# The convolution of a two-layer trunk: the four-token products moved behind the first rows' gates, gates fixed among the taps, six diagonal taps, and empty products in the norm's wait

## The chip, the core and the metric

The kernel runs on one core of a Trainium2 chip. Five engines work beside each other, each through its own queue and in that queue's order: PE (matrix products; its weight loads are shown as PEld), DVE (vector), ACT (scalar), POOL (GpSimd) and SP, which issues most of the transfers. They wait for each other through semaphores only. The time is that of the whole program on the device, in microseconds (us). Three runs of the kernel before took 942.58, 945.01 and 945.92 us; the median, 945.01 us, is the time before.

## The reference, cut to what matters

The program is a two-layer encoder trunk on 256 tokens of 1024 channels in float32. Each layer is a half-weighted gated feed-forward part, a token mixer, and a second such part. The mixer of layer 0 is a convolution module, the only part that the change touches:

```python
def conv_module(h, w_pw1, w_dw, g_norm, w_pw2):
    u = h @ w_pw1
    a, b = jnp.split(u, 2, axis=-1)
    u = a * jax.nn.sigmoid(b)
    u = lax.conv_general_dilated(          # causal, depthwise, 31 taps
        u, w_dw[:, None, :].astype(u.dtype), window_strides=(1,),
        padding=[(CONV_WIDTH - 1, 0)], ...
        feature_group_count=D_MODEL)
    u = jax.nn.silu(rmsnorm(u, g_norm))    # the norm runs over the 1024 channels
    return u @ w_pw2
```

The norm of a token needs all 1024 channels of that token, so nothing behind the norm can start before the slowest channel is convolved.

## The kernel before

**Tiles.** Channels lie on the 128 partitions: eight channel tiles, numbered 0 to 7, each 128 channels by 256 tokens. The tokens are two "rows blocks" of 128, called first rows (tb = 0) and second rows (tb = 1). `V` holds the gated input of the taps, `Y` their sum, `Z` the normed and activated result, and `o` the last product.

**The stage, in order.** `conv_in` goes through a list `steps` of (tile, tokens): tiles 0 and 1 first rows, 0 and 1 second rows, tiles 2 to 5 all tokens, then tiles 6 and 7 first rows, 6 and 7 second rows. A step is two groups of eight matmuls (`gate`, then `u`, line 730), a sigmoid of `gate` on ACT (`sg`, line 739) and a multiplication on DVE (line 750) that writes `V`. I call that multiplication the tile's gate. The four PSUM banks of the tag "A" hold `gate` and `u` in turn, so a step's products also wait until older banks are read.

**The 31 taps** are shared out by the tables `CONV_DVE`, `CONV_POOL` and `CONV_PE` at the head of the file; an entry is (tile, first tap, end, which rows). On DVE a tap is one multiply-add into one of two PSUM accumulators (`acc`, lines 818 and 820), on POOL it is a product on ACT (`prod`, line 845) and an addition on POOL (line 846), with six `prod` buffers between the two engines. On PE a tap is a product with a diagonal matrix of the tap's weights (`taps_pe`, line 856, out `y`); those matrices are made by ACT during the first feed-forward part. Tile 4 takes another way, here called the four-token products: DVE writes its gated input `vq` in four phases (line 743), a transfer stores it to DRAM, four more fetch it back as `VQ` in another layout, and PE does 36 matmuls of 64 columns (`quad`, line 757). Their result goes back through DRAM in the same manner (`yq`, then `YQ`).

**The norm.** For each tile ACT squares `Y` (`square`, `sq`), and PE sums over channels with one-column products (`total`, `ms`). `normed` then runs a chain over four engines: DVE scales the mean (`msc`, line 891), POOL takes the power (`rc`, line 893), ACT makes a diagonal matrix (`dg`, line 895), PE spreads it (`rb`, line 897), DVE multiplies (`z`, line 903), ACT activates (`Z`, line 905), and the last products `o` follow (line 981, and lines 277, 280, 281 for the tiles whose weights are split in two parts). This is done for the first rows, and for the second rows in the middle of the first rows' last products.

**What sets the order.** The program is written with a scheduling layer that places each engine's instructions by its own estimate of time. `order(a, b)` forces b ahead of a on one engine, and functions marked `urgent` are placed ahead of others. The order on each engine is fixed when the program is built.

Of the kernel before, what the change touches and what calls it, by code (L numbers as in the profile page):

```python
# [11 lines left out]
F32 = mybir.dt.float32  # L12
# [7 lines left out]
P = 128  # L20
# [66 lines left out]
def trunk(ctx: ExitStack, tc: tile.TileContext, x, xt, pos, invf, gains, gfin, wdw, wq,  # L87
# [619 lines left out]
    def conv_in(act, X, make_next):  # L707
# [26 lines left out]

        @urgent
        def glu(i, t, gate, u):
# [3 lines left out]
            if i == CONV_QUAD:  # L740
                v = act.tile([P, PH, QT], F32, tag="vq", name="vq")
                by_phase = lambda a: a.rearrange("p (t f) -> p f t", f=PH)
                nc.vector.tensor_mul(v, by_phase(u[:, t]), by_phase(sg[:, :n]))
# [6 lines left out]
            nc.vector.tensor_mul(V[:, i, PAD + t.start:PAD + t.stop], u[:, t], sg[:, :n])  # L750
# [13 lines left out]
        def back(b):  # L764
# [5 lines left out]
            for g in range(4):  # L770
                nc.sync.dma_start(YQ[32 * g:32 * g + 32], dv[g])

# [13 lines left out]
        for n, (i, t) in enumerate(steps):  # L786
# [8 lines left out]
            if i == CONV_LAST[0] - 1:  # L795
                before = quad(mm)
        last_product = before
# [9 lines left out]
        slot = [0]  # L807

        def taps_dve(k, j0, j1, t, after={}):

            slot[0] ^= 1
            c = slice(slot[0] * S, slot[0] * S + t.stop - t.start)
            out = Y[:, k, t]
            for j in range(j0, j1):
# [6 lines left out]
                if j in after:  # L821
                    order(ins, after[j].ins)
# [7 lines left out]
        def taps_pool(k, j0, j1, t):  # L830
# [3 lines left out]
            if k not in odd:  # L834
                odd[k] = act.tile([P, S], F32, tag="odd", name=uid("odd"))
            y = [(part[k] if k in part else Y[:, k, :])[:, t], odd[k][:, t]]
            for j in range(j0, j1):
# [4 lines left out]
                else:  # L842
# [3 lines left out]
                    nc.gpsimd.tensor_tensor(o, o, p, op=ALU.add)  # L846
            nc.gpsimd.tensor_tensor(y[0], y[0], y[1], op=ALU.add)

        def taps_pe(t, done):

            b = bank("A", "y")
            y = {}
            for i, (k, j0, j1) in enumerate(CONV_PE):
                y[k] = b[:, i * P:(i + 1) * P]
                for j in range(j0, j1):
                    mm = nc.tensor.matmul(y[k], diag[k][:, j - j0, :], V[:, k, j + t.start:j + t.stop],
                                          start=(j == j0), stop=(j == j1 - 1))
                    done.append(mm)
            return y

# [27 lines left out]
        def normed(tb, after=()):  # L888
# [4 lines left out]
            nc.gpsimd.tensor_tensor(rc, ms, neghalf, op=ALU.pow)  # L893
            dg = act.tile([P, P], F32, tag="dg", name=uid("dg"), bufs=2)
            nc.scalar.activation(dg, ident, AF.Copy, scale=rc)
# [13 lines left out]
            return on_dve[0], zi  # L909

        halves = (tbs(0), tbs(1), every)
        for items, taps in ((CONV_DVE, taps_dve), (CONV_POOL, taps_pool)):
            for k, j0, j1, half in items:
                if half is not None:
                    taps(k, j0, j1, halves[half])
# [470 lines left out]
```

## Time and profile before

| | |
|---|---|
| median of three runs | 945.01 us |
| the profiled execution's own time | 945.98 us |
| its span (first to last instruction) | 944.2 us |
| mean granted clock of PE | 0.987 |
| PE busy | 924.9 us, 98% |
| DVE, ACT, POOL busy | 679.8, 533.1, 220.4 us |
| convolution stage, from its first product to the first product of the next part | 187.3 to 305.0 us |

Times in rows of the profile are microseconds from the span's start. A row of the timeline gives the start, the time until its last instruction ends, the engine, the line, the operation, what it writes and reads, the shape, and how many records were merged; in brackets stands how long the engine had been idle just before and what ended that wait. A float32 matmul of lines 730, 757, 856, 875 and 981 leaves two records. A row of the stage table gives a stretch, its length, then for each of PE, PEld, DVE, ACT and POOL the busy time with the number of records, then the clock granted to PE (1.00 is full speed, 0.50 half), the share of the transfer engines that was busy, and GB/s.

### The profile page before, as it was taken

How to read it: one execution, taken by the hardware profiler on the slowest of the kernel's cores; microseconds unless marked ns; L12 is line 12 of the kernel's file. 1: busy time of each engine (PE TensorE's matmuls, PEld its weight loads, DVE VectorE, ACT ScalarE, POOL GpSimd, SP SyncE). 2: the span in 40 equal slices, each digit the busy share in tenths (PEclk: the TensorE clock that was granted, in tenths of full speed). 3: DMA queues.
4: the chain of work that ended last, by engine and by line, in shares of the span. 5: the costliest groups of instructions: out<-in, count | busy, mean ns of one | idle time of the engine just before them, and what ended most of it. 6: DMA issues, size and time to landing. Idle time of an engine off the chain costs nothing.

```text
span 944.2 us, 12585 instructions
## 1 busy us (share of the span) xinstructions
PE 924.9 (98%) x4401; PEld 769.6 (82%) x4401; DVE 679.8 (72%) x1042; ACT 533.1 (56%) x927; POOL 220.4 (23%) x337
## 2 busy tenths in 40 slices
PE   8999999998989999999999999999999999999997
PEld 6888887897966888888778888888888778888886
DVE  5866877689665766777786767779675566666875
ACT  6754546478375645546564554554765575454652
POOL 1102232379560000123130102222300001003223
PEclk9999999999789999999999999999999999999999
DMA  9985656666024677655658765667451547675651
GB/s 342 358 288 179 223 158 222 230 218 234 22 90 177 228 242 240 226 164 201 227 205 311 251 226 183 191 211 257 158 222 62 179 166 258 224 249 164 203 209 45
DMA packets 61983, 194.46 MB, mean 206 GB/s; under 512 B 12384, under 2 KB 34784, under 8 KB 42208
## 3 DMA queue, kind: packets, MB, share of 16 engines
q1 hardware_dynamic: 61344, 192.98, 59.2%
q8 instruction: 34, 0.56, 0.2%
q10 hardware_dynamic: 576, 0.69, 0.2%
q14 instruction: 29, 0.24, 0.1%
HBM read 180.79 MB, written 12.85 MB: 205 GB/s over the span
## 4 chain that ended last, share of the span: by engine, by line
PE 69%; DMA 10%; DVE 9%; ACT 4%; issue 4%; POOL 3%; SPq 1%; POOLq 0%; ACTq 0%; DVEq 0%
PE u L277 15%; PE u L281 15%; PE u L280 15%; DVE lo L168 4%; PE o L277 4%; PE o L280 4%; PE o L281 4%; DMA raw<-in_f1w 3%; POOL sums L178 3%; DMA gb<-gd 2%; PE o L981 2%; DMA raw<-in_f2w 2%; PE quad L757 1%; ACT hi L167 1%; DVE lo L187 1%
## 5 line engine op out<-in xcount | busy, mean ns | idle before, releaser
L168 DVE TENSOR_TENSOR lo<-raw,hi 128x1024 fp32r<-128x1024 f32 (+1 forms) x250 | 302.4, 1244 | 81.7 <-ACT hi L167 81.2
L167 ACT CAST hi<-raw 128x1024 fp32r<-128x1024 f32 (+1 forms) x250 | 247.7, 1046 | 152.2 <-PE u L281 107.0
L277 PE MATMUL u<-lo,Xh 128*128 128x512 f32 x688 | 268.1, 390 | 0.7 <-DVE lo L168 0.7
L281 PE MATMUL u<-hi,Xl 128*128 128x512 f32 x688 | 267.8, 390 | 0.9 <-DVE Xl L336 0.9
L280 PE MATMUL u<-hi,Xh 128*128 128x512 f32 x688 | 267.7, 389 | 0.0
L281 PEld LDWEIGHTS u<-hi,Xl 128*128 128x128 f32 x688 | 129.1, 188 | 28.7 <-DVE Xl L336 1.7
L277 PEld LDWEIGHTS u<-lo,Xh 128*128 128x128 f32 x688 | 129.1, 188 | 28.1 <-DVE lo L168 1.1
L280 PEld LDWEIGHTS u<-hi,Xh 128*128 128x128 f32 x688 | 129.1, 188 | 26.4
L277 PE MATMUL o<-lo,Gh 128*128 128x512 f32 (+1 forms) x236 | 91.6, 388 | 1.6 <-DVE lo L168 1.5
L178 POOL TENSOR_TENSOR sums<-raw 128x1024 f32<-128x1024 f32 x20 | 53.3, 2665 | 162.4 <-DMA raw<-in_f2w 43.6
L280 PE MATMUL o<-hi,Gh 128*128 128x512 f32 (+1 forms) x236 | 91.0, 386 | 0.0
L281 PE MATMUL o<-hi,Gl 128*128 128x512 f32 (+1 forms) x236 | 91.0, 386 | 0.0
L617 POOL TENSOR_TENSOR sx<-gb 128x128 f32<-128x128 f32 x20 | 12.1, 603 | 316.7 <-DMA gb<-gd 316.7
L609 ACT CAST Gh<-gb 128x512 fp32r<-128x512 f32 (+2 forms) x48 | 25.7, 538 | 63.7 <-DMA gb<-gd 63.7
L186 ACT CAST hi<-sums 128x1024 fp32r<-128x1024 f32 x40 | 41.2, 1052 | 32.5 <-PE u L281 13.6
L187 DVE TENSOR_TENSOR lo<-sums,hi 128x1024 fp32r<-128x1024 f32 x40 | 56.1, 1434 | 0.0
L610 DVE TENSOR_TENSOR Gl<-gb,Gh 128x512 fp32r<-128x512 f32 (+2 forms) x48 | 33.2, 704 | 31.6 <-ACT Gh L609 31.6
L277 PEld LDWEIGHTS o<-lo,Gh 128*128 128x128 f32 x236 | 44.3, 188 | 12.4 <-DVE lo L168 3.7
L281 PEld LDWEIGHTS o<-hi,Gl 128*128 128x128 f32 x236 | 44.3, 188 | 9.0
L280 PEld LDWEIGHTS o<-hi,Gh 128*128 128x128 f32 x236 | 44.3, 188 | 8.6
L820 DVE SCALAR_TENSOR_TENSOR acc<-V,dw,acc 128x128 f32<-128x128 f32 (+1 forms) x153 | 50.2, 401 | 0.0
L845 ACT ACTIVATE prod<-V,dw 128x128 f32<-128x128 f32 (+1 forms) x131 | 47.0, 410 | 3.0 <-POOL odd L846 1.5
(254 smaller groups left out, 1345.2 us busy)
## 6 DMA issues: line engine op xcount, KB each, us to landing
raw<-in_f2w SPq DMA_DIRECT2D x66, 1024.0 KB, 5.0
raw<-in_f1w SPq DMA_DIRECT2D x64, 1024.0 KB, 5.3
raw<-in_cw SPq DMA_DIRECT2D x12, 1024.0 KB, 6.3
gd<-gt SPq DMA_DIRECT2D x160, 64.0 KB, 2.8
gb<-gd SPq DMA_DIRECT2D x40, 256.0 KB, 2.9
raw<-in_wo SPq DMA_DIRECT2D x4, 1024.0 KB, 5.4
raw<-in_wuq SPq DMA_DIRECT2D x3, 1024.0 KB, 4.8
WQ<-in_wq SPq DMA_DIRECT2D x1, 2304.0 KB, 9.2
```

The costliest lines, as they stand in the source:

```text
L167: behind(nc.scalar.copy(hi[:, c], raw[:, c]))
L168: behind(nc.vector.tensor_sub(lo[:, c], raw[:, c], hi[:, c].bitcast(F32)))
L178: behind(nc.gpsimd.tensor_tensor(t[:, 0:2, :], v[:, 0:4:3, :], v[:, 1:2, :].to_broadcast([P, 2, 512]), op=ALU.add))
L186: behind(nc.scalar.copy(hi[:, c0:c1], x[:, c0:c1]))
L187: behind(nc.vector.tensor_sub(lo[:, c0:c1], x[:, c0:c1], hi[:, c0:c1].bitcast(F32)))
L277: mm = nc.tensor.matmul(o, ah, bl, start=start, stop=False)
L280: nc.tensor.matmul(o, ah, bh, start=False, stop=False)
L281: return nc.tensor.matmul(o, al, bh, start=False, stop=stop)
L609: nc.scalar.copy(dh, x)
L610: nc.vector.tensor_sub(dl, x, dh.bitcast(F32))
L820: ins = nc.vector.scalar_tensor_tensor(out if j == j1 - 1 else y, v, w, y, op0=ALU.mult, op1=ALU.add)
L845: last_prod[0] = nc.scalar.activation(p, v, AF.Copy, scale=w)
```

## The change

Five things are changed, all within the convolution stage:

1. The 36 four-token products stand behind the products of tiles 6 and 7 for the first rows, where they stood ahead of them. The six diagonal taps of tile 6 for the first rows follow them at once.
2. The tables are new. Tile 0's first rows go to DVE whole (31 taps, 22 before), and POOL's nine taps of it with the addition that joined them are gone. Tile 7 has no diagonal taps any more: DVE takes 23 taps and POOL 8 in the first rows, DVE all 31 in the second. PE keeps the six diagonal taps of tile 6. ACT makes six diagonal matrices instead of twelve.
3. `CONV_GATES` ties three gates to places among DVE's taps: the gate of tile 4 ahead of tap 22 of tile 2, those of tiles 6 and 7 (first rows) ahead of taps 10 and 18 of tile 5.
4. `filled` issues 12 empty products (zeros, bfloat16, 256 columns) between the first rows' sums and `rb`, and 6 between `rb` and the last products.
5. In the second rows, ACT's products from the seventh tap on stand behind `dg`, and their additions on POOL behind `rc`. The two accumulators are no longer used in alternating halves, and tiles 6 and 7 have a second buffer for POOL's odd taps.

On PE, from the last products of tile 5 on (`gate_1837`, `u_1838`), before:

```order
L730 MATMUL u_1838<-Xp_1535,raw_1782 128x256 x8
L757 MATMUL quad_1858<-VQ,WQ 128x64 x36
L730 MATMUL gate_1903<-Xp_1535,raw_1805 128x128 x8
L730 MATMUL u_1904<-Xp_1535,raw_1805 128x128 x8
L730 MATMUL gate_1924<-Xp_1535,raw_1835 128x128 x8
L730 MATMUL u_1925<-Xp_1535,raw_1835 128x128 x8
```

and now (`u_1831` is tile 5's):

```order
L732 MATMUL u_1831<-Xp_1528,raw_1775 128x256 x8
L732 MATMUL gate_1851<-Xp_1528,raw_1798 128x128 x8
L732 MATMUL u_1852<-Xp_1528,raw_1798 128x128 x8
L732 MATMUL gate_1872<-Xp_1528,raw_1828 128x128 x8
L732 MATMUL u_1873<-Xp_1528,raw_1828 128x128 x8
L761 MATMUL quad_1893<-VQ,WQ 128x64 x36
L793 MATMUL y_1938<-V,diag_445 128x128 x6
L732 MATMUL gate_1945<-Xp_1528,raw_1798 128x128 x8
```

Four groups of products now stand between tile 5 and the four-token products, and the first rows' diagonal taps have moved up from the end of the stage.

On PE at the norm of the first rows (`ms_2511` and `ms_2514` are the first rows' sums), before:

```order
L856 MATMUL y_2538<-V,diag_445 128x128 x6
L856 MATMUL y_2538<-V,diag_518 128x128 x6
L875 MATMUL ms_2511<-ones,sq_2552 128x1
L875 MATMUL ms_2511<-ones,sq_2555 128x1
L897 MATMUL rb_2565<-dg_2563,ones 128x128
L981 MATMUL o_2697<-raw_1989,Z 128x512
```

and now, up to the first of the empty products:

```order
L793 MATMUL y_2528<-V,diag_445 128x128 x6
L896 MATMUL ms_2514<-ones,sq_2510 128x1
L896 MATMUL ms_2516<-ones,sq_2510 128x1
L896 MATMUL ms_2514<-ones,sq_2512 128x1
L896 MATMUL ms_2514<-ones,sq_2536 128x1
L896 MATMUL ms_2516<-ones,sq_2512 128x1
L896 MATMUL ms_2514<-ones,sq_2539 128x1
L782 LDWEIGHTS still
L782 MATMUL y_2528<-still 128x256
```

The squares of the four-token tile (`sq_2510`) and of tiles 5, 6 and 7 are now summed right behind the second rows' diagonal taps; eleven more empty products, `rb` and six more follow ahead of `o`.

On ACT around the first rows' diagonal matrix, before:

```order
L845 ACTIVATE prod_2690<-V,dw 128x128
L845 ACTIVATE prod_2693<-V,dw 128x128
L895 ACTIVATE dg_2563<-ident,rc_2561 128x128
L905 ACTIVATE Z<-z_2567,G 128x128
L905 ACTIVATE Z<-z_2570,G 128x128
```

and now:

```order
L743 ACTIVATE sg_1984<-gate_1966 128x128
L830 ACT_TABLE_LOAD
L830 ACTIVATE silu_1987<-neghalf 128x1
L890 ACTIVATE sq_2510<-YQ 128x256
L890 ACTIVATE sq_2512<-Y 128x256
L890 ACTIVATE sq_2536<-Y 128x128
L890 ACTIVATE sq_2539<-Y 128x128
L916 ACTIVATE dg_2559<-ident,rc_2557 128x128
L876 ACTIVATE prod_2647<-V,dw 128x128
L876 ACTIVATE prod_2650<-V,dw 128x128
L876 ACTIVATE prod_2653<-V,dw 128x128
L876 ACTIVATE prod_2656<-V,dw 128x128
```

Three more such products follow, and only then the first `Z`: seven products of the second rows have moved from ahead of `dg` to a place between it and `Z`, and the last gate's sigmoid and the table load now stand directly ahead of the four squares.

The diff, cut to its core:

```diff
-CONV_DVE = ((0, 0, 22, 0), (0, 0, 31, 1), (2, 0, 31, 2), (3, 22, 31, 2), (5, 0, 31, 2), (7, 0, 25, None))
-CONV_POOL = ((0, 22, 31, 0), (1, 0, 31, 0), (1, 0, 31, 1), (3, 0, 22, 2), (6, 0, 25, None))
-CONV_PE = ((6, 25, 31), (7, 25, 31))
+CONV_DVE = ((0, 0, 31, 0), (0, 0, 31, 1), (2, 0, 31, 2), (3, 22, 31, 2), (5, 0, 31, 2), (7, 0, 23, 0), (7, 0, 31, 1))
+CONV_POOL = ((1, 0, 31, 0), (1, 0, 31, 1), (3, 0, 22, 2), (6, 0, 25, 0), (7, 23, 31, 0), (6, 0, 25, 1))
+CONV_PE = ((6, 25, 31),)
+
+CONV_GATES = {2: {22: 4}, 5: {10: 6, 18: 7}}
...
+        ybanks = {}
+
+        def filled(n, after):
+
+            for _ in range(n):
+                mm = nc.tensor.matmul(ybanks[P][:, S:], still[:, :P], still, start=True, stop=True)
+                order(mm, after.ins)
+            return mm
...
-            if i == CONV_LAST[0] - 1:
+            if (i, t.start) == (CONV_LAST[-1], 0):
                 before = quad(mm)
+                y[0] = taps_pe(tbs(0), done[0], before)
+                before = done[0][-1]
...
-                if j in after:
-                    order(ins, after[j].ins)
+                for a in [after[j]] if j in after else []:
+                    order(ins, a.ins)
+                if j in CONV_GATES.get(k, ()):
+                    order(ins, gated[CONV_GATES[k][j], 0].ins)
...
-                    nc.gpsimd.tensor_tensor(o, o, p, op=ALU.add)
+                    ins = nc.gpsimd.tensor_tensor(o, o, p, op=ALU.add)
+                    if "power" in after and j >= j0 + 6:
+                        order(last_prod[0], after["diagonal"].ins)
+                        order(ins, after["power"].ins)
...
             a = add()
-            ms, z = normed(tb, (after_row,))
-            steps_of.update({0: a, 4: ms, 9: z})
+            if tb == 0:
+                after_row = filled(12, sums[0])
+            ms, pw, dg, z = normed(tb, (after_row,))
+            if tb == 0:
+                filled(6, brow[0])
+            steps_of.update({0: a, 4: ms, 9: z, "power": pw, "diagonal": dg})
...
-        ends(0, done[1][n // 2 + 1], done[1][n * 3 // 4 + 1])
+        ends(0, done[1][1], done[1][n - 1])
```

More of the change, by code (lines that the diff above doesn't have):

```diff
@@ L733, in products @@
             return mm
+        gated = {}
         @urgent
@@ L771, in back, with taps_pe @@
                 nc.sync.dma_start(YQ[32 * g:32 * g + 32], dv[g])
+        ybanks = {}
[4 more added lines that the diff above has]
+            return mm
+        def taps_pe(t, done, after=None):
+            ybank = ybanks[t.start] = bank("A", "y")
+            y = {}
+            for i, (k, j0, j1) in enumerate(CONV_PE):
+                y[k] = ybank[:, i * P:(i + 1) * P]
+                for j in range(j0, j1):
+                    mm = nc.tensor.matmul(y[k], diag[k][:, j - j0, :], V[:, k, j + t.start:j + t.stop],
+                                          start=(j == j0), stop=(j == j1 - 1))
+                    if after is not None:
+                        order(mm, after.ins)
+                    done.append(mm)
+            return y
+        y, done = {}, {0: [], 1: []}
         def made(k, t):
```

47 lines of the change are left out of this document (19 added, 28 removed).

## The prediction

> **What bounds the kernel now.** I read the page first: PE is busy for 98% of the span, so what counts is where PE waits and where its granted clock is low. The row of slices shows one dip.
>
> ```profile
> PE 924.9 (98%) x4401; PEld 769.6 (82%) x4401; DVE 679.8 (72%) x1042; ACT 533.1 (56%) x927; POOL 220.4 (23%) x337
> ...
> PEclk9999999999789999999999999999999999999999
> ```
>
> The stretches table then shows that the dip has two parts, both in the convolution stage: 13.65 us and 6.83 us at half clock, each behind a stretch in which PE did little.
>
> ```profile
> 229.67:233.08 3.41, 1.48 (x7) 0.95 (x5) 3.38 (x10) 3.05 (x9) 3.41 (x6) 1.00 0.15 35
> 233.08:236.50 3.42, 2.68 (x24) 2.71 (x25) 3.39 (x10) 2.58 (x6) 3.42 (x6) 1.00 0.95 303
> 236.50:250.15 13.65, 13.65 (x66) 13.65 (x66) 9.17 (x24) 1.85 (x5) 5.88 (x9) 0.50 0.04 14
> 270.63:274.04 3.41, 1.14 (x9) 0.86 (x8) 1.49 (x7) 2.23 (x6) 3.41 (x9) 1.00 0.00 0
> 274.04:277.45 3.41, 2.59 (x3) 1.17 (x4) 3.41 (x16) 3.04 (x11) 1.48 (x4) 0.50 0.03 7
> 277.45:280.87 3.42, 3.42 (x5) 1.35 (x4) 3.42 (x15) 0.77 (x3) 0.00 (x0) 0.50 0.00 0
> ```
>
> Both low stretches begin with a wait, which the timeline of PE shows.
>
> ```profile
> 227.53 3.62 PE L730 MATMUL u<-Xp,raw 128*128 128x256 f32 x16
> 233.82 13.16 PE L757 MATMUL quad<-VQ,WQ 128*128 128x64 f32 x72 [2.68 <-DMA VQ<-vqd]
> 246.78 3.62 PE L730 MATMUL gate<-Xp,raw 128*128 128x128 f32 x16
> 250.23 1.95 PE L730 MATMUL u<-Xp,raw 128*128 128x128 f32 x16
> ...
> 260.95 1.95 PE L730 MATMUL u<-Xp,raw 128*128 128x128 f32 x16
> 262.74 1.84 PE L875 MATMUL ms<-ones,sq 128*128 128x1 f32 x16
> 264.44 1.81 PE L856 MATMUL y<-V,diag 128*128 128x128 f32 x14
> ...
> 270.78 0.50 PE L875 MATMUL ms<-ones,sq 128*128 128x1 f32 x4
> 273.48 0.49 PE L897 MATMUL rb<-dg,ones 128*128 128x128 f32 x2 [2.20 <-ACT dg L895]
> ...
> 274.86 10.10 PE L981 MATMUL o<-raw,Z 128*128 128x512 f32 x16 [0.90 <-ACT Z L905]
> ...
> 291.63 7.03 PE L981 MATMUL o<-raw,Z 128*128 128x512 f32 x16
> ```
>
> First, PE has nothing to do from 231.15 (227.53 + 3.62) until `VQ` lands. The four-token products then run mostly at half clock, and the next group takes 3.45 us (246.78 to 250.23) against 1.79 us for its like: six groups lie between 250.23 and 260.95. Second, the norm's chain makes PE wait 2.20 and 0.90 us, and `o` takes 10.10 us where the second rows' `o` takes 7.03. The other engines wait for PE meanwhile:
>
> ```profile
> 241.89 0.73 POOL L847 TENSOR_TENSOR part<-part,odd 128x256 f32<-128x256 f32 x1
> 253.68 0.46 POOL L846 TENSOR_TENSOR part<-part,prod 128x128 f32<-128x128 f32 x1 [11.06 <-ACT prod L845]
> ...
> 261.95 0.46 POOL L846 TENSOR_TENSOR part<-part,prod 128x128 f32<-128x128 f32 x1
> ...
> 266.25 0.46 POOL L847 TENSOR_TENSOR part<-part,odd 128x128 f32<-128x128 f32 x1
> ...
> 272.44 0.55 POOL L893 TENSOR_TENSOR rc<-msc,neghalf 128x1 f32<-128x1 f32 x1
> ```
>
> POOL stands idle for 11.06 us before its taps of tile 6, because that tile's gate waits for the slow products. Its merge at 266.25 releases the first rows' addition at 268.37 (below).
>
> **The change, step by step.**
>
> *The four-token products.* Four groups of 1.79 us, 7.15 us, now stand ahead of them, so PE reaches them at 231.15 + 7.15 = 238.3. `VQ` was there at 233.8, and the gate that feeds it keeps its place in DVE's row (`vq` below, at 226.95), so 4.5 us are to spare: the wait of 2.68 us goes. Tiles 6 and 7's weights are now wanted at 231.15 and 234.7, 15 us sooner. They are issued at 219.28 and just behind, and the transfer engines are nearly idle from 229 on, so they have landed by then, with at least 2 us to spare.
>
> ```profile
> 219.28 0.80 SPq L155 DMA_DIRECT2D raw<-in_cw  x2
> 227.00:229.00 2.00, 2.00 (x11) 1.77 (x10) 2.00 (x6) 1.64 (x5) 2.00 (x5) 1.00 0.89 351
> 229.00:231.00 2.00, 2.00 (x10) 1.54 (x9) 1.97 (x6) 1.64 (x4) 2.00 (x4) 1.00 0.06 22
> 226.95 0.60 DVE L743 TENSOR_TENSOR vq<-u,sg 128x256 f32<-128x256 f32 x1
> ```
>
> At full clock the 72 records take 72 x 0.112 = 8.0 us (24 took 2.68 us at full clock), where they took 12.96 (233.82 to 246.78): 4.9 us less. The group behind saves 1.66 us. PE is at the end of them at 246.3, of tile 6's six first-row taps (12 records, 1.34 us) at 247.7, and of the last four groups at 254.8, where it was at 262.74.
>
> *The taps.* DVE gets 9 + 4 taps in the first rows, 13 x 0.27 = 3.5 us (eleven take 2.93 below). Nine come where DVE still has waits of its own, four behind the last gates. POOL loses nine early additions and gains eight at the end. The six second-row taps of tile 7 that DVE takes from PE are not on the way to the first rows' sums. The six diagonal matrices left out of ACT's first part cost and save nothing, since PE bounds that part; at most 6 x 0.4 = 2.4 us would be gained.
>
> *The first rows' sums.* PE could sum at 254.8 + 1.7 (`ms`, 262.74 to 264.44) + 1.34 = 257.9. But POOL, free at 242.6 with tile 6's gate done before, has 24 additions for tile 6 and 7 for tile 7; 0.414 us each (20 steps from 253.68 to 261.95). Twenty-eight of them, the merge of tile 6 and four of tile 7 among them, end at 242.6 + 11.6 = 254.2, against 266.7 for the merge before.
>
> ```profile
> 268.37 0.29 DVE L952 TENSOR_TENSOR Y<-y,part 128x128 f32<-128x128 f32 x1 [4.87 <-POOL odd L846]
> 259.75 2.93 DVE L820 SCALAR_TENSOR_TENSOR acc<-V,dw,acc 128x128 f32<-128x128 f32 x11
> 192.44 2.14 ACT L845 ACTIVATE prod<-V,dw 128x128 f32<-128x128 f32 x7
> 261.61 1.28 ACT L799 ACT_TABLE_LOAD   x1
> 264.47 0.65 ACT L869 ACTIVATE sq<-YQ 128x256 f32<-128x256 f32 x1
> 269.11 0.29 ACT L869 ACTIVATE sq<-Y 128x128 f32<-128x128 f32 x1
> 273.02 0.40 ACT L895 ACTIVATE dg<-ident,rc 128x128 f32<-128x128 f32 x1 [0.52 <-POOL rc L893]
> 274.41 1.57 ACT L905 ACTIVATE Z<-z,G 128x128 f32<-128x128 f32 x5 [0.98 <-DVE z L903]
> ```
>
> Behind that merge ACT is the late one. DVE adds and gates tile 6's second rows by 254.8 (twice 0.29). ACT then has six products and the last sigmoid (7 x 0.29 = 2.0), the table load (1.28) with its small `silu` (0.2), the squares of `YQ` (0.65) and of three tiles (3 x 0.3): 259.8. With 0.5 for the summing products the sums end at 260.3; before, at 271.28 (270.78 + 0.50). That is 11.0 us less, and it holds all that the four-token products saved and the wait for POOL besides. DVE's eight remaining taps of tile 7 and two additions end by 257.7 and are covered.
>
> *The norm's chain.* `rc` had stood behind POOL's additions until 272.44, about 0.9 us; its way is free now. But seven products (2.0 us) stand ahead of `Z` on ACT, where `rb` and `z` needed 0.99 us (273.42 to 274.41): 1.05 us more. Together +0.2: `o` begins near 264.1. The empty products run in waits that are longer than they are, so they delay nothing.
>
> *`o` itself* takes 10.10 - 7.03 = 3.1 us less if the clock stays full. It may not. Between 257.9 and 264.1 PE's dense work is the 18 empty products (23 such took 4.30 us at the program's cold start, so about 0.1 each at full clock) and `rb`, some 2.2 us. A stretch of 3.41 us can hold as little as 1.3 of it. One with 1.48 us kept the clock, one with 1.14 lost it. I take back 0.9 of the 3.1, from bounds of none and 3.1.
>
> ```profile
> 1.04 4.30 PE L269 MATMUL warm<-still 128*128 128x256 bf16 x23 [1.04 <-DVE still L264]
> ```
>
> Sum: -11.0 + 0.2 - 3.1 + 0.9 = -13.0 us. Behind the stage PE keeps its order, and it is busy throughout, so the gain lasts to the end. The profiled execution took 945.98 us, 0.97 above the median of the runs; from it the sum gives 933.0, from the median 932.0. I say **932.5 us**.
>
> **The rivals.**
>
> *The clock falls on the four-token products.* The fall at 236.50 came at the end of a stretch that held 2.68 us of these very 64-column products, and three more stretches of them (236.50 to 246.78) did not bring it back. If they are too thin by themselves, moving them changes nothing of that. For it: the stretch with 1.48 us of ordinary products kept the clock. Against: the stretch that fell also held 0.74 us of nothing. Price: one stretch of the 13.65 us is saved, 10.2 us stay at half, 5.1 us of work lost; PE has 1.9 us to spare before the squares (257.9 to 259.8): 3.2 us, so 935.7.
>
> The Trainium skill bears on this: its page "TensorE: Matmul & The Clock Gate", section "Why this matters for your kernels", says that only PE-idle gaps above some 3 us between bursts of matmuls bring the clock down. By it the 2.68 us gap would have been harmless and the thin products the culprit, which is this rival's 935.7. The page's Part 1 gives a window of 3413 ns; here the trace agrees (13.65 and 6.83 us are four and two of them). It also wants a whole idle window, and there the trace differs: the window that fell was busy for 2.68 of its 3.42 us.
>
> *A new wait at the norm.* The last gates on PE wait for sigmoids that ACT can only reach behind POOL-paced products; by the sum above the last sigmoid comes about when PE does, with 0.2 us to spare. The same holds for the second rows, whose products were held back behind `dg`: their sum is wanted at 273.7 and is ready by about 273.2. If ACT or POOL runs 10% late there, over 31 additions and as many activations, 3 to 5 us of the gain goes: 936 to 938.
>
> *Slower than before.* POOL now sets the end. If its additions, beside 13 more taps on DVE, lost their pace, the whole stage would follow. This decides from 13.0/31 = 0.42 us more per addition on, a doubling, and then gives 945 and above. Against it: beside DVE's taps they took 0.46 us without exception in the rows above.
>
> **How the numbers follow.** The forecast, with the clock full or nearly so, has 0.70 (its own range 930 to 934.7); the thin products 0.15; the late ACT or POOL 0.09; slower 0.03; and 0.03 that the two halves of the dip return elsewhere and the time stays within 0.3% (2.8 us, about what a measurement tells from no change). The range reaches from 929, where the clock never falls and DVE's and ACT's small terms come out low, to 938, the late case's end. Faster by over 0.3%: 0.94, within: 0.03, slower: 0.03.
>
> **What the profile after would show.** Right: no PE wait for `VQ`; the four-token products in about 8 us near 238; no dip there; the first rows' sums near 260; POOL without the 11 us wait; the first product of the next part near 292 where it was at 305. Wrong: half clock within the four-token products; a PE wait above 1 us at tile 7's last `u`; `o` again at 10 us; POOL additions above 0.5 us. What would undo the forecast is a clock that falls for thin products rather than for waits.

## The result, and the profile after

The changed kernel took 931.03 us (median of four executions, 930.70 to 932.47) where the kernel before, run beside it, took 945.46 us (942.58 to 946.16). The ratio is 0.9856, with a 95% interval of 0.9833 to 0.9879: 14.4 us, or 1.4%, faster. A second comparison on another occasion gave 931.43 us, ratio 0.9866 (0.9809 to 0.9923). The forecast was 932.5 us. Of the 57 executions of the kernel before that ran beside the experiments, six took 936.8 to 937.8 us at a mean granted clock of 0.994 to 0.996, and the other 51 took 942.4 to 948.4 us at 0.985 to 0.988.

The page of the changed kernel's profile (span 929.1 us, own time 930.93) no longer has a dip in its row of clocks, and PE's busy time fell by 10 us with nearly the same number of products:

```profile
PE 914.9 (98%) x4395; PEld 762.9 (82%) x4395; DVE 686.8 (74%) x1053; ACT 532.2 (57%) x920; POOL 221.0 (24%) x336
...
PEclk9999999999999999999999999999999999999999
```

PE's timeline of the convolution stage, from the last products of tile 5 to the first product of the next part:

```profile
225.92 3.62 PE L732 MATMUL u<-Xp,raw 128*128 128x256 f32 x16
...
236.52 8.15 PE L761 MATMUL quad<-VQ,WQ 128*128 128x64 f32 x72
244.50 1.56 PE L793 MATMUL y<-V,diag 128*128 128x128 f32 x12
...
251.93 2.05 PE L732 MATMUL u<-Xp,raw 128*128 128x128 f32 x16 [0.29 <-ACT sg L743]
253.81 1.84 PE L896 MATMUL ms<-ones,sq 128*128 128x1 f32 x16
...
259.38 1.50 PE L896 MATMUL ms<-ones,sq 128*128 128x1 f32 x12 [2.28 <-ACT sq L890]
260.74 2.59 PE L782 MATMUL y<-still 128*128 128x256 bf16 x12
263.13 0.64 PE L918 MATMUL rb<-dg,ones 128*128 128x128 f32 x2
...
264.68 7.13 PE L1009 MATMUL o<-raw,Z 128*128 128x512 f32 x16
...
291.59 0.40 PE L279 MATMUL u<-lo,Xh 128*128 128x512 f32 x1
```

There is no wait for `VQ`, and the 72 records of the four-token products run at full clock. What is new is a wait of 2.28 us for the squares `sq` ahead of the first rows' last sums. The stage table shows the one low stretch that is left, behind a stretch that held 1.53 us of work:

```profile
257.50:260.91 3.41, 1.53 (x14) 1.52 (x15) 1.88 (x7) 2.52 (x6) 0.52 (x2) 1.00 0.69 284
260.91:264.33 3.42, 3.42 (x18) 2.57 (x17) 1.99 (x9) 2.56 (x9) 2.31 (x6) 0.50 0.00 0
264.33:267.74 3.41, 3.41 (x11) 1.55 (x10) 3.41 (x16) 3.41 (x12) 2.10 (x6) 1.00 0.02 5
```

To compare executions that reach the stage at different times, I take its length: from the first record of tile 0's `gate` to the first record of the part behind it (`u`, 291.59 above), and what lies behind that to the end of the span. All profiles of this study, in us (a low clock at the very end, behind PE's work, is left out):

| kernel | tile 0's first product | first `o` | next part's first product | stage | behind it | low clock in the stage |
|---|---|---|---|---|---|---|
| before | 187.28 | 274.86 | 304.98 | 117.7 | 639.2 | 13.7 + 6.8 |
| before_again | 185.63 | 272.87 | 302.50 | 116.9 | 638.6 | 13.7 + 6.8 |
| before_third | 185.84 | 273.25 | 303.09 | 117.3 | 639.1 | 13.7 + 6.8 |
| after | 185.67 | 264.68 | 291.59 | 105.9 | 637.6 | 3.4 |
| after_again | 185.93 | 266.25 | 293.44 | 107.5 | 637.5 | 6.8 |
| quad_only | 185.76 | 266.35 | 295.85 | 110.1 | 639.2 | 6.8 |
| gap_filled | 185.74 | 269.34 | 298.35 | 112.6 | 639.1 | 6.8 |
| quad_back | 185.40 | 272.18 | 299.31 | 113.9 | 637.5 | 17.1 + 3.4 |
| no_empty | 185.79 | 264.72 | 293.69 | 107.9 | 640.2 | 6.8 |
| no_empty_again | 185.44 | 264.52 | 294.47 | 109.0 | 641.7 | 10.2 |
| empty_thin | 185.38 | 264.37 | 293.38 | 108.0 | 637.5 | 6.8 |
| pool_adds | 185.69 | 261.25 | 288.16 | 102.5 | 637.6 | none |
| square_late | 185.59 | 273.21 | 300.86 | 115.3 | 637.5 | 3.4 + 13.7 |
| z_sooner | 185.56 | 260.16 | 288.40 | 102.8 | 637.5 | none |

So 11.8 of the 15.05 us between the two first profiles (945.98 and 930.93) come from the stage, and 1.6 us from behind it, in work that the change does not touch. Another 1.6 us lay ahead of the stage, in the first profile of the kernel before and in no other. The experiments take these apart.

### The profile page after: what moved, and what is told of

It reads as the page before. It is cut to its first block, busy times and chain, and to the rows that moved or that the text cites. A ratio compares the mean times of both kernels' runs of the same rounds, so it can differ in the third digit from the quotient of the medians.

```text
span 929.1 us, 12574 instructions
## 1 busy us (share of the span) xinstructions
PE 914.9 (98%) x4395; PEld 762.9 (82%) x4395; DVE 686.8 (74%) x1053; ACT 532.2 (57%) x920; POOL 221.0 (24%) x336
## 4 chain that ended last, share of the span: by engine, by line
PE 84%; DVE 5%; ACT 4%; DMA 2%; issue 2%; POOL 2%; SPq 0%; POOLq 0%; ACTq 0%; DVEq 0%
PE u L283 17%; PE u L282 17%; PE u L279 17%; PE o L279 6%; PE o L282 6%; PE o L283 6%; DVE lo L170 3%; PE p L283 2%; PE p L282 2%; PE p L279 2%; ACT hi L169 2%; PE o L1009 1%; DMA raw<-in_cw 1%; POOL odd L877 1%; DMA raw<-in_f1w 1%
## 5 line engine op out<-in xcount | busy, mean ns | idle before, releaser
L849 DVE SCALAR_TENSOR_TENSOR acc<-V,dw,acc 128x128 f32<-128x128 f32 (+1 forms) x166 | 53.7, 396 | 0.0
```

The lines of the kernel that those rows point to most:

```text
L849: ins = nc.vector.scalar_tensor_tensor(out if j == j1 - 1 else y, v, w, y, op0=ALU.mult, op1=ALU.add)
```

## The experiments

### The move alone

quad_only is the kernel before with one line changed:

```diff
-            if i == CONV_LAST[0] - 1:
+            if (i, t.start) == (CONV_LAST[-1], 0):
                 before = quad(mm)
```

> The kernel before with one edit: the four-token products stand behind the first rows' gates of tiles 6 and 7. Tables of taps, twelve diagonal matrices and the norm stay as they were. My theory (the wait for VQ and the low clock behind it are what was lost, and POOL then sets the end of the first rows' sums): the wait of 2.68 us goes, the products take 8.0 us, POOL's merge of tile 6 comes near 255.7 instead of 266.7 and the first rows' sums near 260.3: 933 to 936 us. Rival (the gain sits in the new tables of taps): above 938 us. Rival (the thin products lower the clock by themselves): half clock within them again, about 940 us.

Measured: 936.09 us (934.20 to 937.00), ratio 0.9913 (0.9882 to 0.9944). PE's timeline of it:

```profile
236.61 8.15 PE L757 MATMUL quad<-VQ,WQ 128*128 128x64 f32 x72
...
261.66 0.50 PE L875 MATMUL ms<-ones,sq 128*128 128x1 f32 x4
264.66 0.80 PE L897 MATMUL rb<-dg,ones 128*128 128x128 f32 x2 [2.50 <-ACT dg L895]
266.35 3.78 PE L981 MATMUL o<-raw,Z 128*128 128x512 f32 x4 [0.89 <-ACT Z L905]
```

The products take 8.15 us at full clock and the first rows' last sum ends at 262.16, 76.4 us after tile 0's first product, where it ended 84.0 us after it (271.28 less 187.28). The stage is 7.6 us shorter than in the first profile of the kernel before: about two thirds of the stage's whole gain come from the move alone. The norm's waits and the half clock of `o` are still there. The sums came 3.4 us later than expected (76.4 us after tile 0's first product, against 73.0 by the forecast), and the time lies just above the expected 933 to 936 us. POOL's merge of tile 6 did not hold them up, it ended at 251.20; ahead of the last square ACT still made twelve products of the second rows (257.62 to 261.22), and ahead of the last sum PE still ran 15 diagonal taps (258.23 to 261.83).

### The wait or the thin products

gap_filled leaves the order of the kernel before and fills PE's wait for `VQ`:

```diff
             b = bank("A", "quad")
+            for _ in range(25):
+                gap = nc.tensor.matmul(b[:, S:2 * S], still[:, :P], still, start=True, stop=True)
+                order(gap, after.ins)
+            after = gap
             for g in range(4):
```

> The kernel before with one addition: 25 empty bf16 products between the last u of tile 5 and the four-token products, which fill PE's wait for VQ and shorten nothing. If waiting brought the clock down, it stays full now: four-token products 8.0 us instead of 12.96, the group behind them 1.79 instead of 3.45, everything behind 6.6 us earlier, 939 us (936 to 940, the low end if the norm's half clock goes as well). If the thin 64-column products bring it down, it falls as before: 945 us within 1.

Measured: 938.85 us, ratio 0.9959 (0.9930 to 0.9987). Seven of ten executions took 936.8 to 939.3, three 944.0 to 946.2. The profiled one (939.28) shows the same thin products, at nearly the same place as before, at full clock, though 0.55 us of the wait is left:

```profile
229.44 2.89 PE L756 MATMUL quad<-still 128*128 128x256 bf16 x25
232.88 8.22 PE L761 MATMUL quad<-VQ,WQ 128*128 128x64 f32 x72 [0.55 <-DMA VQ<-vqd]
```

So without most of the wait the clock stays full, and the rival (the products are too thin by themselves) is out: quad_only, gap_filled and the changed kernel hold the full clock through 8 us of them. The three executions near 945 us were not profiled, but their mean granted clock was 0.986 to 0.987, against 0.992 to 0.996 in the other seven. So the clock fell in them too; that it fell here, over the rest of the wait, is likely and not shown.

That the wait alone decides is not shown either. The prediction says that PE did little in the stretch ahead of the fall, but in all three profiles of the kernel before that stretch was busy for more than half its length, with the thin products behind the wait: 2.68 us in the first, and in the other two

```profile
230.13:233.54 3.41, 2.01 (x18) 2.04 (x19) 3.38 (x10) 2.81 (x7) 3.41 (x7) 1.00 0.75 240
```

```profile
231.01:234.42 3.41, 2.33 (x21) 2.36 (x22) 3.38 (x10) 2.75 (x7) 3.41 (x6) 1.00 0.79 270
```

A stretch of ordinary and empty products with 2.22 us kept the clock in pool_adds (last section). So the thin products may count for less while PE waits, though they hold a full clock by themselves. And the wait does not always cost the clock: the six executions of the kernel before near 937 us had a mean clock about 0.008 above the others. Estimated from that, they lost 7.5 us less to half clock (0.008 of 940 us), which is nearly the whole of their lead (937.3 us in the mean, against a median of 945.1). They were not profiled; that it was the fall at the four-token products that they were spared is the likely reading.

### The move undone

quad_back is the changed kernel with the four-token products ahead of the first rows' gates again, and everything else new:

```diff
+            if i == CONV_LAST[0] - 1:
+                before = quad(mm)
             if (i, t.start) == (CONV_LAST[-1], 0):
-                before = quad(mm)
-                y[0] = taps_pe(tbs(0), done[0], before)
+                y[0] = taps_pe(tbs(0), done[0], mm)
```

> The changed kernel with the four-token products put back ahead of the first rows' gates; tables of taps, places of gates, empty products stay new. Theory: the wait for VQ and the half clock return, POOL waits 11 us again and its additions for tiles 6 and 7 start near 252, so that the first rows' sums come near 269.5; only the o at full clock stays of the gain: 938 to 942 us. Rival (the tables and empty products carry the gain): below 935 us.

Measured: 938.97 us, ratio 0.9934 (0.9899 to 0.9970). Five of seven executions took 938.6 to 940.1, two 930.7 and 932.0. The profiled one (938.63) shows PE's row and the stretches around the fall:

```profile
230.87 14.88 PE L761 MATMUL quad<-VQ,WQ 128*128 128x64 f32 x72 [1.60 <-DMA VQ<-vqd]
```

```profile
228.24:231.65 3.41, 1.81 (x12) 1.39 (x11) 3.38 (x10) 3.06 (x9) 3.41 (x6) 1.00 0.52 91
231.65:235.06 3.41, 3.41 (x18) 3.41 (x18) 3.38 (x10) 2.57 (x6) 3.41 (x6) 0.50 0.63 259
...
241.89:245.30 3.41, 3.41 (x18) 3.41 (x18) 0.00 (x0) 0.00 (x0) 0.00 (x0) 0.50 0.00 0
245.30:248.72 3.42, 3.42 (x18) 3.42 (x18) 0.00 (x0) 0.69 (x2) 0.00 (x0) 0.50 0.11 38
```

A wait of 1.60 us was enough, together with the first thin products behind it. Five stretches at half clock followed. The first four were full of the thin products (18 records each): they do not bring a full clock down, but once it is down they did not bring it back. The thin products end at 245.75, so the fifth is mostly the group of 128 columns behind them, and after it the clock was full. The two executions near 931 us had a mean granted clock of 0.998 and 0.997, against 0.988 to 0.990 in the other five, and they took as long as the changed kernel (931.03 us). So with the new tables the price of the old order is the clock, and hardly the wait itself: the move pays by keeping the clock. The two were not profiled, so where their clock stayed full is argued.

### The empty products

no_empty leaves the 18 empty products out; empty_thin keeps them as instructions and cuts them to one column:

```diff
-            if tb == 0:
-                after_row = filled(12, sums[0])
...
-            if tb == 0:
-                filled(6, brow[0])
```

```diff
-                mm = nc.tensor.matmul(ybanks[P][:, S:], still[:, :P], still, start=True, stop=True)
+                mm = nc.tensor.matmul(ybanks[P][:, S:S + 1], still[:, :P], still[:, :1], start=True, stop=True)
```

> The changed kernel without its 18 empty products (they compute nothing that is used). In the changed kernel's trace the clock fell at 260.91 anyway and was full again at 264.33, behind a stretch that the empty products had filled. Theory: without them a second stretch, 264.3 to 267.7, runs at half clock, 1.7 us of o lost: 932.5 us or a little above. Rival: at half clock the empty products only hold up rb (dg was there at 262.14, rb began at 263.13), so leaving them out gains up to 0.9 us: 930 us.

Measured: 935.60 us (934.37 to 935.72), ratio 0.9907 (0.9883 to 0.9931): 4.6 us slower than the changed kernel, more than either idea gave. PE's timeline:

```profile
262.38 0.80 PE L918 MATMUL rb<-dg,ones 128*128 128x128 f32 x2 [1.31 <-ACT dg L916]
264.72 9.20 PE L1005 MATMUL o<-raw,Z 128*128 128x512 f32 x16 [1.54 <-ACT Z L926]
```

`rb` runs 0.75 us sooner, so the empty products do hold it up; but `Z` stands behind seven products on ACT either way, and `o` begins at the same time (264.72 against 264.68). It then takes 9.20 us instead of 7.13. That is 2.0 us in the stage. The other 2.6 us are behind it, in a feed-forward part, though the order on every engine is the same there. POOL's and SP's timelines of no_empty, then POOL's of the changed kernel at the same block:

```profile
625.01 2.40 POOL L180 TENSOR_TENSOR sums<-raw 128x1024 f32<-128x1024 f32 x1 [8.57 <-DMA raw<-in_f1w]
```

```profile
618.32 0.33 SPq L177 DMA_DIRECT2D raw<-in_f1w  x1
```

```profile
619.18 2.39 POOL L180 TENSOR_TENSOR sums<-raw 128x1024 f32<-128x1024 f32 x1 [7.08 <-DMA raw<-in_f1w]
```

The block that POOL waits for was issued at 618.32, and POOL could begin 6.7 us later; in the changed kernel it was 5.2 us (issued at 613.99). In no_empty's transfer records one 16 KB packet of an instruction queue (q8 on the page) starts at 620.52, within the block; in the changed kernel's it starts at 613.07, ahead of the block. The queue carries 34 such packets in the program. Two more kernels test whether the number of PE's instructions decides where the packet falls.

> The changed kernel without its empty products once more. Its first profile lost 2.0 us in the stage (o at half clock) and 2.6 us behind it to one late weight block. If the late block was chance, the part behind the stage takes 637.5 to 639 us now and the time is 933 us; if it belongs to this program, 640.2 and 935.6 us again. The stage stays at 107.9 us within 0.7.

Measured: 935.33 us, ratio 0.9908 (0.9877 to 0.9938); the profiled execution took 937.97. The packet is at 620.48, the block is late again, and the part behind the stage takes 641.7 us. That is more than the first time: the clock fell there too, for one stretch from 632.47 on. The stage took 109.0 us, with a third stretch at half clock, a little outside the expected 107.9 within 0.7.

> The changed kernel with its 18 empty products cut from 256 columns to 1: as many instructions on PE, next to no work. It parts two things that went together when they were left out: the clock in the norm (2.0 to 3.1 us in the stage) and the late weight block behind the stage (2.6 us and more in both profiles), in which a packet of an instruction queue, 16 KB, came in the middle of the block. If the place of that packet hangs on the number of PE's instructions, the part behind the stage takes 637.5 us again while the stage stays at 107.9 to 109: 933.0 us (932.3 to 934.0). If the late block comes of the missing work or the clock, it stays: 935.5 us.

Measured: 932.57 us (931.93 to 933.12), ratio 0.9860 (0.9843 to 0.9876). PE's and POOL's timelines:

```profile
260.58 0.44 PE L782 MATMUL y<-still 128*128 128x1 bf16 x12
...
264.37 9.21 PE L1009 MATMUL o<-raw,Z 128*128 128x512 f32 x16 [1.41 <-ACT Z L926]
```

```profile
620.69 2.40 POOL L180 TENSOR_TENSOR sums<-raw 128x1024 f32<-128x1024 f32 x1 [6.93 <-DMA raw<-in_f1w]
```

The stage is that of no_empty (108.0 against 107.9), and the part behind it that of the changed kernel (637.5). So the empty products are worth 2.0 us as work, by the clock of `o`, and 2.6 us as 36 more instructions on PE (18 products and 18 weight loads). That these act by moving the instruction packets against the weight blocks is read from the packets' places and was not tested by itself. The Trainium skill, page "Runtime: NRT & Kernel Launch", section "Instruction fetch mechanics", says that a sequencer fetches its instructions in 16 KiB blocks through a DMA queue of its own, mostly hidden. The size agrees with the traces for the queue q8; here the packet of 0.95 us (1.95 in the second profile) was, by this reading, not hidden, since it came within a block that a chain of four engines waited for.

### Is the part ahead of and behind the stage chance

> The kernel before, a second profile of it. In the first one PE lost about 1.6 us ahead of the convolution and 1.7 us behind it to weight casts that came late, which the changed kernel's profile has not. If that is chance from one execution to the next, these places look different here, while the convolution stage (first product of tile 0 to the first product of the next part) takes 117.7 us again, within 1.

> The kernel before, a third profile, for the same question: 638.6 to 639.2 us behind the stage again if the late block belongs to this program, as little as 637.5 if it is chance. The stage takes 117.3 us, within 1, as long as the clock falls at the four-token products.

> The changed kernel once more. Its first profile took 637.56 us from the first product behind the convolution stage to the end, the kernel before 639.22 and 638.62 for the same unchanged work, where a weight block that landed late held up POOL's sum and DVE's cast by 0.7 to 1.8 us in a feed-forward part. If such late blocks fall by chance, this profile may show one and then 638 to 640 us there; if the changed program never has them, 637.5 again. The stage itself takes 105.9 us, within 0.7, either way, or 2 us less where the norm keeps the full clock.

Measured: 942.91 and 944.02 us for the two executions of the kernel before, 931.43 us for the changed kernel (profiled execution 932.75). The 1.6 us ahead of the stage did not come again (185.63 and 185.84 against 187.28): they were chance. Behind the stage the kernel before takes 638.6 to 639.2 us in all three profiles, and the changed kernel 637.5 in both. In each of the three profiles of the kernel before a packet of the same queue lies within a weight block of a feed-forward part. In the first one the block was issued at 450.58 and the packet starts at 453.49; POOL's timeline has the block's landing:

```profile
456.73 2.41 POOL L178 TENSOR_TENSOR sums<-raw 128x1024 f32<-128x1024 f32 x1 [8.04 <-DMA raw<-in_f2w]
```

In the other two the packets start at 450.45 and 449.50, in blocks issued at 447.93 and 448.42, and the landings are as late. So the 1.1 to 1.7 us belong to the program, as a side effect of its number of instructions and not of its new order. The table above bears this out. The part behind the stage takes 637.5 to 637.6 us in all seven profiles whose page counts 4395 records of products on PE, quad_back with the old order among them. It takes 638.6 to 639.2 us in all four with 4401, quad_only with the new order among them. gap_filled, with 25 products more than the kernel before, takes 639.1 us as well, but the packet and the late block are elsewhere: the block issued at 897.96, with a packet at 898.93. So the loss moves with the packets, and more instructions do not always mean a longer time. The second profile of the changed kernel spent two stretches at half clock in the norm instead of one, and its stage took 107.5 us, against the 105.9 within 0.7 that I expected. The same program's stage so varies by 1.6 us, as one stretch at half clock or two fall into the norm.

### DVE and POOL keep each other waiting

The changed kernel's stage holds one thing that no step of the prediction has. Its DVE timeline has a plain addition of 128x256 that takes 3.13 us:

```profile
243.06 3.13 DVE L940 TENSOR_TENSOR Y<-Y,part 128x256 f32<-128x256 f32 x1 [0.73 <-POOL part L881]
...
251.39 3.45 DVE L849 SCALAR_TENSOR_TENSOR acc<-V,dw,acc 128x128 f32<-128x128 f32 x13
254.74 0.28 DVE L976 TENSOR_TENSOR Y<-y,part 128x128 f32<-128x128 f32 x1
254.94 0.28 DVE L754 TENSOR_TENSOR V<-u,sg 128x128 f32<-128x128 f32 x1
```

Beside it POOL's timeline shows additions without a pause until 245.91, then a pause, and ACT's a wait of 2.35 us for the same addition:

```profile
242.28 0.75 POOL L881 TENSOR_TENSOR part<-part,odd 128x256 f32<-128x256 f32 x1
242.96 0.48 POOL L877 TENSOR_TENSOR part<-part,prod 128x128 f32<-128x128 f32 x1
...
245.43 0.48 POOL L877 TENSOR_TENSOR part<-part,prod 128x128 f32<-128x128 f32 x1
247.08 0.46 POOL L877 TENSOR_TENSOR odd<-odd,prod 128x128 f32<-128x128 f32 x1 [1.17 <-ACT prod L876]
...
252.87 0.48 POOL L881 TENSOR_TENSOR part<-part,odd 128x128 f32<-128x128 f32 x1
```

```profile
246.23 0.42 ACT L890 ACTIVATE sq<-Y 128x256 f32<-128x256 f32 x1 [2.35 <-DVE Y L940]
...
255.26 0.40 ACT L872 ACTIVATE part<-V,dw 128x128 f32<-128x128 f32 x1 [3.38 <-DVE V L754]
```

In the kernel before, the same addition took 0.43 us, with POOL idle beside it, as DVE's timeline and POOL's pause of 11.06 us from 242.62 on (in the prediction) show:

```profile
242.65 0.43 DVE L919 TENSOR_TENSOR Y<-Y,part 128x256 f32<-128x256 f32 x1 [0.55 <-POOL part L847]
```

Two kernels test the reading that POOL's additions keep DVE from its operands. pool_adds gives the addition to POOL; square_late makes POOL's run longer by moving one activation, ACT's squares of tile 3, behind the first rows' products, so that ACT feeds POOL without a pause:

```diff
-                nc.vector.tensor_add(Y[:, k, t], Y[:, k, t], part[k][:, t])
+                nc.gpsimd.tensor_add(Y[:, k, t], Y[:, k, t], part[k][:, t])
```

```diff
-        late = (CONV_QUAD, CONV_LAST[0] - 1)
+        late = (3, CONV_QUAD, CONV_LAST[0] - 1)
```

> The changed kernel with one addition moved from DVE to POOL, Y of tile 3 plus POOL's part of it (128x256). In the changed kernel's trace DVE's row of it took 3.13 us, as long as POOL added without a pause beside it, where the kernel before had 0.43 us with POOL idle; ACT's square waited 2.35 us for it and POOL 1.17 us for ACT. Theory (the two engines kept each other from their operands): the 3.13 us row is gone, POOL spends 0.7 us instead of waiting 1.17, the first rows' sums come 0.4 to 1.2 us sooner: 930.3 us (929.8 to 930.7). Rival (only the record is long, nothing waited for it): 931.0 us.

Measured: 927.85 us (927.49 to 929.67), ratio 0.9833 (0.9807 to 0.9860): 3 us faster than the changed kernel, its range apart from that kernel's, and more than expected. POOL's row, then PE's:

```profile
243.73 0.73 POOL L940 TENSOR_TENSOR Y<-Y,part 128x256 f32<-128x256 f32 x1
```

```profile
256.20 1.40 PE L896 MATMUL ms<-ones,sq 128*128 128x1 f32 x12
257.45 1.47 PE L782 MATMUL y<-still 128*128 128x256 bf16 x12
...
261.25 7.13 PE L1009 MATMUL o<-raw,Z 128*128 128x512 f32 x16 [1.20 <-ACT Z L926]
```

The wait of 2.28 us for the squares is gone, the sums end at 257.60 instead of 260.88, and the clock never falls in the stage. I had counted POOL's 1.17 us and not DVE's 2.7 us: DVE's whole row behind the addition was late, so that tile 6's merge (252.87 + 0.48) lay finished for 1.4 us before DVE came to add it (254.74), and tile 6's second gate, ACT's products, the last sigmoid and the squares stood behind that.

> The changed kernel with one activation in another place: the squares of tile 3 stand on ACT behind the last product of the first rows, no longer ahead of nine of them. ACT so feeds POOL without a pause while DVE's addition of tile 3 (3.13 us in the changed kernel) waits to run. If POOL's additions keep DVE from its operands, that row now lasts until POOL first pauses, 8 to 10 us, DVE's gates and taps behind it come 5 us late, and the time is 935 to 940 us. If the row is long for a reason of its own, it stays at 3.1 us and ACT's wait of 2.35 us is gone: 930 us.

Measured: 939.68 us (938.39 to 941.47), ratio 0.9953 (0.9936 to 0.9970): slower than the changed kernel by more than 8 us. DVE's and POOL's timelines:

```profile
243.06 10.16 DVE L940 TENSOR_TENSOR Y<-Y,part 128x256 f32<-128x256 f32 x1 [0.72 <-POOL part L881]
```

```profile
252.44 0.50 POOL L877 TENSOR_TENSOR odd<-odd,prod 128x128 f32<-128x128 f32 x1
253.02 0.52 POOL L881 TENSOR_TENSOR part<-part,odd 128x128 f32<-128x128 f32 x1
```

One addition of DVE lasted 10.16 us, through POOL's whole run. It ended at 253.22, 0.28 us behind the start of POOL's first pause (252.94 to 253.02); in the changed kernel it ended at 246.19, also 0.28 us behind the start of the pause (245.91). The introduction says that the engines wait for each other through semaphores only; this wait has no semaphore, and the profile shows it as a long busy instruction, not as idle time in brackets. The Trainium skill, page "SBUF — State Buffer", section "SBUF: two separate sides", says that a DVE instruction with two inputs in SBUF and a GpSimd instruction that reads SBUF need the same pair of ports, and that whichever starts first has it for its whole instruction. The traces agree on which instructions collide: DVE's additions with one input in PSUM (`Y<-acc,Y`, line 857) took 0.42 us in the midst of POOL's run. They go further on the length: DVE waited not for one instruction of 0.49 us but for some 24 in a row. Not all of the 9.4 us by which the stage is longer is DVE's wait: in square_late the clock was at half for 17.1 us of the stage, in the changed kernel for 3.4.

### Z ahead of more products

z_sooner starts from pool_adds. The second rows' products of the seventh to ninth tap still stand behind `dg`; those from the tenth tap on now stand behind the first `Z`. The core of its edit:

```diff
-                        order(last_prod[0], after["diagonal"].ins)
+                        order(last_prod[0], after["diagonal" if j < j0 + 9 else "first Z"].ins)
```

> The kernel with POOL's addition of tile 3, in which ACT now makes the first Z behind three, not seven, of the second rows' products. There PE waited 1.20 us for Z. Expected: o begins 0.9 us sooner, and the second rows' sums, whose dg was the late one by 0.2 us, hold up the second rows' o by 0.4 to 0.6 us: 927.5 us (927.0 to 928.0) against 927.85. If the second rows have room, 927.0 or less; if they have none, no change or slower.

Measured: 929.30 us (927.71 to 932.33), ratio 0.9855 (0.9827 to 0.9884): no gain over pool_adds. `o` begins 1.1 us sooner, and PE then waits for the second rows' squares, as its timeline shows:

```profile
260.16 7.13 PE L1011 MATMUL o<-raw,Z 128*128 128x512 f32 x16 [0.25 <-ACT Z L926]
...
271.41 0.61 PE L896 MATMUL ms<-ones,sq 128*128 128x1 f32 x4 [1.32 <-ACT sq L890]
```

The second rows had no room: ACT has hardly a pause from 258.32 to 268.0, and what `Z` gains its products lose. They feed POOL's additions and DVE's last sum, for which ACT's last square then waits 2.06 us.

## Why the prediction was right, and where it was not

**The four-token products** came as told: 50.9 us after tile 0's first product (51.0 forecast), without a wait, 8.15 us at full clock. The theory behind it, that the clock falls with the wait and not for thin products by themselves, stands after quad_only and gap_filled; the rival of 935.7 us is out. Whether the thin products behind a wait help to bring it down is open. The transfers past which the step was moved were no trouble.

**The six diagonal matrices** cost and saved nothing: tile 0's first product came at 185.4 to 185.9 us in every profile but one, with six or with twelve.

**The first rows' sums** are the step that failed, by 2.2 us. The prediction had them end 73.0 us after tile 0's first product (260.3 less 187.28); they ended after 75.2 (260.88 less 185.67). Where it says "DVE adds and gates tile 6's second rows by 254.8" it takes DVE's row as being on time. DVE had lost 2.7 us to one addition beside POOL's run, and was done with that add and gate at 255.22, which is 256.8 on the time base of the prediction (this execution reaches the stage 1.6 us sooner): 2 us late. That is the term of the sum that was mis-sized: -8.8 us where -11.0 stands. With the collision gone (pool_adds) the sums end after 71.9 us. The slower rival had the right two engines and looked at the wrong one: it asked whether DVE's taps slow POOL's additions, and these kept their 0.46 to 0.49 us.

**The norm's chain**: +0.2 forecast, and from the end of the sums to `o` it took 3.80 us (260.88 to 264.68) against 3.58 (271.28 to 274.86). "They delay nothing" was right for `o` and wrong for `rb`, which the empty products held up by 0.75 us at half clock.

**`o`**: the clock fell for one stretch, from 260.91 to 264.33, which ended before `o` began; `o` took 7.13 us, 2.97 less than before where the sum has 2.2 (3.1 less 0.9). In the second profile two stretches were low, and the norm's chain took the loss: `o` began 1.3 us later after tile 0's first product (80.3 against 79.0), and took 7.39. Taking something back was right, but the loss did not fall on `o`.

**What the sum left out.** The stage gained 11.8 us from the first profiles, where 13.0 was forecast; over all profiles of the two kernels it is 10.6 (117.3 less 106.7). The time gained 13.3 to 14.4 us, because the part behind the stage became 1.1 to 1.7 us shorter, which no step had, and because executions of the kernel before differ by some 2 us ahead of and behind the stage. So the mechanism was right, but that the forecast of 932.5 us came within 1.5 us is in part luck: the stage gained 1.2 to 2.4 us less than forecast, and gains ahead of and behind it, which the forecast does not have, hid this.

A second thing that the sum took for granted is the clock of the kernel before. In six of its 57 executions the time was near 937 us, and against those the changed kernel gains some 6 us, not 14.

In sum, of the changed kernel's stage 7.6 us come from the move (quad_only), 2.2 from all the rest of the change but the empty products (the tables of taps, the gates' places, the products held back behind `dg`; quad_only to no_empty, 110.1 to 107.9), and 2.0 from the empty products. No run parts the 2.2 us further, and they are little more than the 1.6 us by which two profiles of one program differ. Giving one addition to another engine gained 3.4 us more of the stage (105.9 to 102.5).

## What to carry to other kernels

When PE is busy 98% of the time, look for the stretch at half clock and for the wait just ahead of it, and put other products into the wait rather than thicker ones behind it. Then compare several executions: the same kernel can keep the clock in some and lose it in others. Before an engine's row is taken as "on time" in a sum, look for its instructions that share something with a neighbour which the change will make busier: here an addition that cost 0.43 us beside an idle POOL cost 3.13 and 10.16 us beside a busy one. When a time moves in a part whose order did not change, compare the number of instructions ahead of it before blaming the step under study.

## What was not expected of the hardware

- DVE's addition with both inputs in SBUF got no turn in some 24 back-to-back additions of POOL (10.16 us), while POOL's own additions stayed at 0.49 to 0.50 us.
- The clock fell behind stretches of 3.41 us that held 1.53 and 1.81 us of PE's busy time; it stayed full behind 2.22 us of busy time in pool_adds, as its stage table shows. No one limit of busy time parts the cases: it stayed full behind 1.48 us in the kernel before, and fell there behind 2.01 to 2.68 us with 64-column products, and behind 2.37 us in quad_back's norm (265.79 to 269.20). At half clock, stretches full of 64-column products did not bring it back (four in a row in quad_back, three in the kernel before), while one stretch of 128-column products did (245.30 to 248.72 in quad_back), and one full of the norm's work and empty products did too (260.91 to 264.33 in the changed kernel).

```profile
259.01:262.43 3.42, 2.22 (x11) 1.37 (x12) 2.64 (x12) 3.42 (x13) 3.14 (x8) 1.00 0.03 12
```

- 36 instructions fewer on PE shifted the instruction packets, and the part behind the stage became 2.6 us longer, with a packet of 16 KB within a late weight block 360 us behind the place of the edit.
